# A decoder block on one core: the first norm's sums of squares are taken by ACT from token rows, and the first chunk's loads are cut anew

## The chip, the cores and the metric

The kernel runs on one NeuronCore of a Trainium2 chip. The metric is the device time of one execution in microseconds (us). Three runs of the kernel before took 1370.49, 1372.42 and 1373.44 us; the median is 1372.42. The names used below are those of the profile: PE is the matrix engine (TensorE), PEld its weight loads, DVE the vector engine, ACT the scalar engine, POOL the GpSimd engine, and SP the engine whose queue issues the transfers.

## The reference

One decoder block over 256 tokens of width 2048, in float32:

```
h = x + token_mixer(rmsnorm(x, norm1_w), ...)     # one input projection, retention and an SSD scan side by side,
                                                  # one output projection
h = h + hier_moe(rmsnorm(h, norm2_w), ...)        # 32 experts in 4 groups, two per token, gated MLPs
return rmsnorm(h, final_norm_w)

def rmsnorm(x, w):
    y = x * rsqrt(mean(x * x, axis=-1) + 1e-6)
    return y * w
```

What matters here is the first `rmsnorm`: for each of the 256 tokens a sum of squares over 2048 channels, and from it one factor per token. The input projection is linear in each token, so the factor can be applied after it.

## The kernel before, in words

Tokens lie in two halves of 128. The 2048 channels are 16 tiles of 128 (KT = 16). The input projection is done in 13 chunks of 512 output columns; each chunk is a loop over the 16 channel tiles. A tile's weights (128 x 512) are split into two float32r parts, a rounded one (`wh`, on ACT) and the rest (`wl`, on DVE), and six products of 512 columns (or twelve of 256) go to PE per tile: wh with xh, wl with xh, wh with xl. The split input (`xh` on ACT, `xl` on DVE, named `twin` for the first eight tiles) is made once, in the first chunk, by `prep_x`; it carries the norm's weight but not the factor per token. Each `wh`/`wl` pair has six buffers (two pools of three, STAGE = 6), so ACT and DVE can be at most six tiles ahead of PE.

Weights come in pieces of 8 tiles (2 MB) into a ring of two buffers (RING_A = 2); the transfer of a chunk's first half therefore waits until DVE has made the last `wl` of the half that lay in that buffer. All transfers stand in one queue, SP's, in order: one that waits holds up those behind it. In the first chunk the two halves are loaded in smaller pieces, each with the piece of x that goes with it (`first_tiles`).

The factor per token is made by `rms1`, which is taken up beside the second chunk by `pump` (a list of pieces of work, one of which is recorded after every second tile). `squares` has POOL square the 16 tiles of x (4 tiles at a time) and add them up; PE sums over the channels (`psr`); DVE and POOL make `rcol`, one factor per token on partitions; DVE and PE spread it over columns (`dg`, `psb`, `rbc`). `keep_v` takes the first chunk's result out of PSUM with `rcol` (ACT, tile `v`).

A scheduler turns this into a fixed order of instructions for each engine; an instruction that waits holds up everything behind it on its engine.

After the 13 chunks come the output projection, the routing, and eight groups of four experts. The experts' weights come in 192 pieces of 2 MB (some 400 MB of the 485 MB that the kernel moves), through rings of 2 MB buffers, on the same SP queue (`wload` and `stream`, L774); a piece is asked for when PE has used up the buffer it goes to.

Of the kernel before, what the change touches and what calls it, by code (L numbers as in the profile page):

```python
# [9 lines left out]
F32 = mybir.dt.float32  # L10
# [3 lines left out]
AF = mybir.ActivationFunctionType  # L14
# [4 lines left out]
P = 128  # L19
D = 2048  # L20
T = 256
NT = T // P
# [15 lines left out]
SPLIT = 1  # L38
# [111 lines left out]
def block_kernel(tc, I, out):  # L150
    nc = tc.nc
    act, dve, pe, pool, sp = nc.scalar, nc.vector, nc.tensor, nc.gpsimd, nc.sync
    MUL, ADD, SUB, MAX, MIN = ALU.mult, ALU.add, ALU.subtract, ALU.max, ALU.min
    EQ = ALU.is_equal

    def tt(o, a, b, op):
        dve.tensor_tensor(o, a, b, op=op)  # L157

    def stt(o, a, s, b, op0, op1, **k):
        dve.scalar_tensor_tensor(o, a, s, b, op0=op0, op1=op1, **k)  # L160

    def ts(o, a, s1, s2, op0, op1=None):
        if op1 is None:
            dve.tensor_scalar(o, a, s1, None, op0=op0)
        else:
            dve.tensor_scalar(o, a, s1, s2, op0=op0, op1=op1)

    def sb(name, side="left", bufs=1, **k):
        return tc.alloc_tile_pool(name=name, bufs=bufs, side=side, **k)
# [3 lines left out]
    par = cp.tile([P, PARAM.n], F32, name="par")  # L173

    def V(name):
        t, (o, n) = (par, PARAM.at[name]) if name in PARAM.at else (mxp, MIXP.at[name])
        return t[:, o:o + n]

    def C(name):
        t, (o, n) = (con, CONST.at[name]) if name in CONST.at else (mxc, MIXC.at[name])  # L180
        return t[:, o:o + n]
# [3 lines left out]
    sm = sb("small")  # L185
# [15 lines left out]
    ones = mp.tile([P, P], F32, name="ones")  # L201
    dve.memset(ones, 1.0)

    def twin(i, n, dt=F32):
        return qp.tile([P, 2, n, 2048 // n], dt, tag=f"h{i}", name=f"twin{i}")

    def t1(name, dt=F32, shape=(P, T)):
        return mp.tile(list(shape), dt, tag="t1", bufs=6, name=name)
# [4 lines left out]
    def misc(shape, name):  # L213
        return pm.tile(shape, F32, tag="pm", name=name)

    def rsqrt_mean(o, ss, n, tag):
        m = sm.tile(list(ss.shape), F32, name="rm" + tag)
        ts(m, ss, 1.0 / n, EPS, MUL, ADD)
        pool.tensor_tensor(o, m, mh[:, :ss.shape[1]], op=ALU.pow)
# [9 lines left out]
    xraw = hp.tile([P, KT, T], F32, tag="h", name="xraw")  # L229
# [3 lines left out]
    n1 = V("n1")  # L233

    def xh(k):
        return xhs[k // 8][:, k % 8]

    def xl(k):
        return xls[k // 8][:, k % 8]

    def load_x(a, b):
        sp.dma_start(xraw[:, a:b], I["xt"][:, a:b])

    def prep_x(a, b):
        for k in range(a, b):
            act.activation(xh(k), xraw[:, k], AF.Copy, scale=n1[:, k:k + 1])
            stt(xl(k), xraw[:, k], n1[:, k:k + 1], xh(k).bitcast(F32), MUL, SUB)

    rcol = cp.tile([P, NT], F32, name="rcol")
    lowb = cp.tile([P, P], BF16, name="lowb")  # L250
    onb = cp.tile([P, P], BF16, name="onb")
    pool.memset(onb, 1.0)
    rbc = mp.tile([P, T], F32, name="rbc")
    sq = t1("sq")

    def squares():

        ab = twin(1, 8)
        a, b = ab[:, 0, :4], ab[:, 1, :4]
        for i in range(4):  # L260
            xr = xraw[:, 4 * i:4 * i + 4]
            pool.tensor_tensor(b if i else a, xr, xr, op=MUL)
            if i:
                pool.tensor_tensor(a, a, b, op=ADD)
        pool.tensor_tensor(a[:, :2], a[:, :2], a[:, 2:], op=ADD)
        pool.tensor_tensor(sq, a[:, 0], a[:, 1], op=ADD)

    def rms1():
        squares()
        yield  # L270

        ps = misc([P, NT], "psr")
        for t in range(NT):
            pe.matmul(ps[:, t:t + 1], sq[:, t * P:(t + 1) * P], ones[:, :1], start=(t == 0), stop=True,
                      skip_group_check=True)
        rsqrt_mean(rcol, ps, D, "1")
        dg = t1("dg", shape=(P, NT, P))
        ps = misc([P, T], "psb")
        for t in range(NT):
            ts(dg[:, t], ident, rcol[:, t:t + 1], None, MUL)  # L280
        pe.matmul(ps, ones, dg.rearrange("p a b -> p (a b)"), start=True, stop=True)
        dve.tensor_copy(rbc, ps)
        yield
        sp.dma_start(mxp, I["mixp"])
        sp.dma_start(mxc, I["mixc"])
        sp.dma_start(wdt[:, :KT], I["wdt"])
        act.activation(lowb, C("strict"), AF.Copy)

    def split(w, n):
        for i in range(0, w.shape[1], n):  # L290
            st = stages.pop(0)
            stages.append(st)
            wh = st.tile([P, n, 512], F32R, tag="wh", name="wh")
            wl = st.tile([P, n, 512], F32R, tag="wl", name="wl")
            act.activation(wh, w[:, i:i + n], AF.Copy)  # L295
            tt(wl, w[:, i:i + n], wh.bitcast(F32), SUB)
            for j in range(n):
                yield i + j, wh[:, j], wl[:, j]

    def load(src):  # L300
        w = ring.tile([P, 8, 512], F32, tag="w", name="w")
        sp.dma_start(w, src)
        return w
# [23 lines left out]
                    pass  # L327

    def first_tiles():
        sp.dma_start(par, I["par"])  # L330
        for i, parts in enumerate((((0, 1), (1, 2), (2, 4), (4, 6), (6, 8)), ((0, 2), (2, 4), (4, 6), (6, 8)))):
            w = ring.tile([P, 8, 512], F32, tag="w", name="w")
            for a, b in parts:
                load_x(8 * i + a, 8 * i + b)
                sp.dma_start(w[:, a:b], I["win"][0, i, :, a:b])
            if i == 1:
                sp.dma_start(con, I["con"])
            for a, b in parts:
                prep_x(8 * i + a, 8 * i + b)
                for j, wh, wl in split(w[:, a:b], SPLIT):  # L340
                    yield 8 * i + a + j, wh, wl

    def win_tiles(ci):
        if ci == 0:
            yield from first_tiles()
            return
        for i in range(2):
            for j, wh, wl in split(load(I["win"][ci, i]), SPLIT):
                yield 8 * i + j, wh, wl

    def form_b(ci):
        ps = [pa.tile([P, 2, T], F32, tag="pa", name="pb") for _ in range(2)]
        for k, wh, wl in win_tiles(ci):
            for c in range(4):
                o = ps[c // 2][:, c % 2]
                s = slice(c * P, (c + 1) * P)
                pe.matmul(o, wh[:, s], xh(k), start=(k == 0 and c % 2 == 0), stop=False, skip_group_check=True)  # L357
                pe.matmul(o, wh[:, s], xl(k), start=False, stop=False, skip_group_check=True)  # L358
                pe.matmul(o, wl[:, s], xh(k), start=False, stop=(k == KT - 1), skip_group_check=True)  # L359
            if k % 2:  # L360
                pump(rate)
        return ps

    def form_a(tiles, lh, ll):
        ps = [pa.tile([P, 512], F32, tag="pa", name="pf") for _ in range(NT)]
        for k, wh, wl in tiles:
            for t in range(NT):
                s = slice(t * P, (t + 1) * P)
                pe.matmul(ps[t], lh(k)[:, s], wh, start=(k == 0), stop=False)  # L369
                pe.matmul(ps[t], lh(k)[:, s], wl, start=False, stop=False)  # L370
                pe.matmul(ps[t], ll(k)[:, s], wh, start=False, stop=(k == KT - 1))  # L371
            if k % 2:
                pump(rate)
        return ps
# [280 lines left out]
    for ci, (n, half) in enumerate(CHUNKS):  # L655
        rate = 2 if (n, half) == ("z", 0) else 1
        if n in ("xs", "bc", "q", "k"):
            ps = form_b(ci)
        else:
            ps = form_a(win_tiles(ci), xh, xl)  # L660
        finish_all(soon)
        if ci == 0:
            soon.append(rms1())
# [88 lines left out]
    op = sb("outp", side="right", reuse_waits="tile")  # L752
# [411 lines left out]
```

## Time and profile before

| | |
|---|---|
| median of 3 runs | 1372.42 us (1370.49 to 1373.44) |
| the profiled execution's own time | 1369.11 us |
| its span | 1367.3 us |
| PE busy | 1051.8 us (77%) |
| DVE busy | 415.9 us (30%) |
| ACT busy | 271.4 us (20%) |
| POOL busy | 25.6 us (2%) |
| DMA | 484.93 MB, mean 355 GB/s |
| mean granted clock of PE | 0.899 of full speed |

The span is what the trace covers; the execution takes 1.8 us more. A row of the timeline view gives a start and a length in us, then engine, line, operation and tile; "x2" means two instructions merged, and a bracket gives the idle time of the engine before it and what ended it. A granted clock of 1.00 is 2.4 GHz, 0.50 is 1.2 GHz.

### The profile page before, as it was taken

How to read it: one execution, taken by the hardware profiler on the slowest of the kernel's cores; microseconds unless marked ns; L12 is line 12 of the kernel's file. 1: busy time of each engine (PE TensorE's matmuls, PEld its weight loads, DVE VectorE, ACT ScalarE, POOL GpSimd, SP SyncE). 2: the span in 40 equal slices, each digit the busy share in tenths (PEclk: the TensorE clock that was granted, in tenths of full speed). 3: DMA queues.
4: the chain of work that ended last, by engine and by line, in shares of the span. 5: the costliest groups of instructions: out<-in, count | busy, mean ns of one | idle time of the engine just before them, and what ended most of it. 6: DMA issues, size and time to landing. Idle time of an engine off the chain costs nothing.

```text
span 1367.3 us, 17274 instructions
## 1 busy us (share of the span) xinstructions
PE 1051.8 (77%) x7323; PEld 597.3 (44%) x7323; DVE 415.9 (30%) x842; ACT 271.4 (20%) x504; POOL 25.6 (2%) x29
## 2 busy tenths in 40 slices
PE   6999999999999997667558567665865766595654
PEld 4889999888787542133113213211320321141112
DVE  8577977665655321011002101100200110020013
ACT  5465544465544100000000000000000000000003
POOL 5000000000000000000000000000000000000000
PEclk9999999999999998789889978978987896798888
DMA  7445555585875999999999999999999999999995
GB/s 264 177 151 189 192 193 202 195 323 193 327 301 223 365 426 427 427 427 427 428 427 426 426 429 426 425 427 428 428 425 427 426 427 428 427 427 426 428 425 222
DMA packets 38723, 484.93 MB, mean 355 GB/s; under 512 B 4561, under 2 KB 5233, under 8 KB 9585
## 3 DMA queue, kind: packets, MB, share of 16 engines
q1 hardware_dynamic: 38642, 483.78, 86.0%
q8 instruction: 59, 0.97, 0.3%
q14 instruction: 22, 0.18, 0.0%
HBM read 481.65 MB, written 2.11 MB: 354 GB/s over the span
## 4 chain that ended last, share of the span: by engine, by line
DMA 63%; PE 34%; DVE 1%; issue 1%; ACT 0%; SPq 0%; POOL 0%; POOLq 0%; DVEq 0%; ACTq 0%
DMA wt<-wexp 39%; DMA twin<-wexp 23%; PE pb L357 4%; PE pb L359 4%; PE pb L358 4%; PE pf L370 3%; PE pf L371 3%; PE pf L369 3%; PE po L729 2%; PE po L727 2%; PE po L728 2%; PE pg L973 1%; PE pu L973 1%; PE pxg L947 1%; DMA w<-win 1%
## 5 line engine op out<-in xcount | busy, mean ns | idle before, releaser
L973 PE MATMUL pu<-wt,xg 128*32 128x512 f32 x864 | 144.3, 798 | 95.9 <-DMA wt<-wexp 95.9
L973 PE MATMUL pg<-wt,xg 128*32 128x512 f32 x832 | 135.7, 782 | 84.3 <-DMA wt<-wexp 84.2
L157 DVE TENSOR_TENSOR wl<-w,wh 128x512 fp32r<-128x512 f32 x224 | 157.9, 717 | 73.0 <-ACT wh L295 71.6
L295 ACT ACTIVATE wh<-w 128x512 fp32r<-128x512 f32 x224 | 139.7, 630 | 149.2 <-PE pb L358 77.0
L157 DVE TENSOR_TENSOR sg<-sg,pu 128x512 f32<-128x512 f32 x8 | 5.5, 688 | 537.5 <-PE pu L973 536.3
L973 PE MATMUL py<-wt,at 128*32 128x128 f32 (+1 forms) x1456 | 112.7, 418 | 19.0 <-DMA wt<-wexp 19.0
L973 PEld LDWEIGHTS pu<-wt,xg 128*32 128x32 f32 x864 | 28.8, 129 | 208.5 <-DMA wt<-wexp 157.3
L973 PEld LDWEIGHTS pg<-wt,xg 128*32 128x32 f32 x832 | 25.8, 127 | 182.5 <-DMA wt<-wexp 136.2
L157 DVE TENSOR_TENSOR acc<-acc,psc 128x128 f32<-128x128 f32 (+1 forms) x98 | 43.3, 459 | 170.4 <-PE psc L1004 170.3
L1004 PE MATMUL psc<-y,swt 128*128 128x128 f32 (+1 forms) x224 | 70.8, 439 | 25.9 <-ACT y L1001 25.1
L973 PEld LDWEIGHTS py<-wt,at 128*32 128x32 f32 x1456 | 42.0, 110 | 78.6 <-issue 35.6
L1001 ACT ACTIVATE y<-py 128x128 f32<-128x128 f32 (+1 forms) x56 | 23.2, 414 | 233.3 <-PE py L973 233.2
L958 ACT ACTIVATE swt<-psw 128x256 f32<-128x256 f32 x8 | 3.1, 383 | 324.6 <-PE psw L956 324.6
L357 PE MATMUL pb<-twin,wh 128*128 128x256 f32 x224 | 64.4, 288 | 0.6 <-ACT wh L295 0.6
L359 PE MATMUL pb<-twin,wl 128*128 128x256 f32 x224 | 64.2, 288 | 0.0
L357 PE MATMUL pb<-xh,wh 128*128 128x256 f32 x224 | 64.2, 286 | 0.0
L358 PE MATMUL pb<-twin,wh 128*128 128x256 f32 x224 | 64.0, 286 | 0.0
L1004 PEld LDWEIGHTS psc<-y,swt 128*128 128x128 f32 x224 | 33.3, 192 | 67.9 <-ACT y L1001 56.3
L947 PEld LDWEIGHTS pxg<-selr,h 128*128 128x128 f32 x512 | 60.0, 196 | 6.5 <-issue 5.9
L359 PE MATMUL pb<-xh,wl 128*128 128x256 f32 x224 | 62.8, 280 | 0.0
L358 PE MATMUL pb<-xl,wh 128*128 128x256 f32 x224 | 62.7, 280 | 0.0
L990 ACT ACTIVATE sg<-pg 128x512 f32<-128x512 f32 x8 | 4.8, 597 | 291.4 <-PE pg L973 291.4
(259 smaller groups left out, 1479.2 us busy)
## 6 DMA issues: line engine op xcount, KB each, us to landing
wt<-wexp SPq DMA_DIRECT2D x156, 2048.0 KB, 39.1
twin<-wexp SPq DMA_DIRECT2D x34, 2048.0 KB, 39.1
w<-win SPq DMA_DIRECT2D x24, 2048.0 KB, 7.9
wt<-wout SPq DMA_DIRECT2D x6, 2048.0 KB, 12.3
w<-wout SPq DMA_DIRECT2D x2, 2048.0 KB, 7.8
wt<-wexp SPq DMA_DIRECT2D x4, 1024.0 KB, 31.9
w<-win SPq DMA_DIRECT2D x7, 512.0 KB, 8.1
de<-acd SPq DMA_DIRECT2D x8, 256.0 KB, 3.3
```

The source lines that it names most:

```text
L157: dve.tensor_tensor(o, a, b, op=op)
L295: act.activation(wh, w[:, i:i + n], AF.Copy)
L357: pe.matmul(o, wh[:, s], xh(k), start=(k == 0 and c % 2 == 0), stop=False, skip_group_check=True)
L358: pe.matmul(o, wh[:, s], xl(k), start=False, stop=False, skip_group_check=True)
L359: pe.matmul(o, wl[:, s], xh(k), start=False, stop=(k == KT - 1), skip_group_check=True)
L369: pe.matmul(ps[t], lh(k)[:, s], wh, start=(k == 0), stop=False)
L370: pe.matmul(ps[t], lh(k)[:, s], wl, start=False, stop=False)
L371: pe.matmul(ps[t], ll(k)[:, s], wh, start=False, stop=(k == KT - 1))
L727: pe.matmul(ps[t], yh[:, s], wh, start=(k == 0), stop=False)
L947: pe.matmul(px[:, i], h[:, t, (k0 + i) * P:(k0 + i + 1) * P], selr[:, t], start=(i == 0 and x == 0), stop=(x == NT - 1), skip_group_check= ...
L973: pe.matmul(ps[s], lhsT[:, s], w(j), **k)
L1004: pe.matmul(px, swt[:, t * P:(t + 1) * P], y, start=True, stop=True)
```

## The change

The tile `sq` and the function `squares` go, and with them POOL's nine large operations at the start and PE's product `psr`. Instead x is loaded a second time, by token rows (`xtok`, 2 MB, 128 partitions x 4096), behind the first weights of the second chunk on SP's queue; ACT squares it in place in four instructions of 128 x 1024, each leaving a sum (`accum_out`) in `ss1`; DVE adds the two halves (`ssum`), and the rest of `rms1` stands as it was.

The first chunk's loads have 12 pieces instead of 18. The parameters (`par`) and the first weight tile are issued by ACT; all others by SP.

```diff
-    def prep_x(a, b):
-        for k in range(a, b):
-            act.activation(xh(k), xraw[:, k], AF.Copy, scale=n1[:, k:k + 1])
-            stt(xl(k), xraw[:, k], n1[:, k:k + 1], xh(k).bitcast(F32), MUL, SUB)
+    def prep_x(k):
+        act.activation(xh(k), xraw[:, k], AF.Copy, scale=n1[:, k:k + 1])
+        stt(xl(k), xraw[:, k], n1[:, k:k + 1], xh(k).bitcast(F32), MUL, SUB)
...
-    sq = t1("sq")
-
-    def squares():
-
-        ab = twin(1, 8)
-        a, b = ab[:, 0, :4], ab[:, 1, :4]
-        for i in range(4):
-            xr = xraw[:, 4 * i:4 * i + 4]
-            pool.tensor_tensor(b if i else a, xr, xr, op=MUL)
-            if i:
-                pool.tensor_tensor(a, a, b, op=ADD)
-        pool.tensor_tensor(a[:, :2], a[:, :2], a[:, 2:], op=ADD)
-        pool.tensor_tensor(sq, a[:, 0], a[:, 1], op=ADD)
+    xtok = twin(1, 1)[:, :, 0]
+    ss1 = sm.tile([P, NT, 2], F32, name="ss1")
+    ssum = sm.tile([P, NT], F32, name="ssum")
 
     def rms1():
-        squares()
-        yield
-
-        ps = misc([P, NT], "psr")
+
         for t in range(NT):
-            pe.matmul(ps[:, t:t + 1], sq[:, t * P:(t + 1) * P], ones[:, :1], start=(t == 0), stop=True,
-                      skip_group_check=True)
-        rsqrt_mean(rcol, ps, D, "1")
+            for i in range(2):
+                row = xtok[:, t, 1024 * i:1024 * i + 1024]
+                act.activation(row, row, AF.Square, accum_out=ss1[:, t, i:i + 1])
+            yield
+
+        tt(ssum, ss1[:, :, 0], ss1[:, :, 1], ADD)
+        rsqrt_mean(rcol, ssum, D, "1")
...
     def first_tiles():
-        sp.dma_start(par, I["par"])
-        for i, parts in enumerate((((0, 1), (1, 2), (2, 4), (4, 6), (6, 8)), ((0, 2), (2, 4), (4, 6), (6, 8)))):
+        for i, parts in enumerate((((0, 1), (1, 2), (2, 4), (4, 8)), ((0, 4), (4, 8)))):
             w = ring.tile([P, 8, 512], F32, tag="w", name="w")
+            if i == 0:
+                act.dma_start(par, I["par"])
             for a, b in parts:
                 load_x(8 * i + a, 8 * i + b)
-                sp.dma_start(w[:, a:b], I["win"][0, i, :, a:b])
+                (sp if i or a else act).dma_start(w[:, a:b], I["win"][0, i, :, a:b])
...
     def win_tiles(ci):
...
         for i in range(2):
-            for j, wh, wl in split(load(I["win"][ci, i]), SPLIT):
+            w = load(I["win"][ci, i])
+            if ci == 1 and i == 0:
+                sp.dma_start(xtok, I["x"])
+            for j, wh, wl in split(w, SPLIT):
                 yield 8 * i + j, wh, wl
```

On SP's queue, around the end of the first chunk's loads, there stood before (`xraw` is x by channels, `w` the weights, 128x4096 is a whole 2 MB piece; L302 is the load of a later chunk's half):

```order
L335 DMA w<-win 128x1024
L242 DMA xraw<-xt 128x512
L335 DMA w<-win 128x1024
L337 DMA con<-con 128x160
L302 DMA w<-win 128x4096
L284 DMA mxp<-mixp 128x108
L285 DMA mxc<-mixc 128x1289
L286 DMA wdt<-wdt 128x256
L302 DMA w<-win 128x4096 x8
```

And now, from the fourth transfer of the queue on (L326 is the first chunk's weights, `twin_126` is `xtok`):

```order
L242 DMA xraw<-xt 128x512
L326 DMA w<-win 128x1024
L242 DMA xraw<-xt 128x1024
L326 DMA w<-win 128x2048
L242 DMA xraw<-xt 128x1024
L326 DMA w<-win 128x2048
L328 DMA con<-con 128x160
L292 DMA w<-win 128x4096
L341 DMA twin_126<-x 128x4096
L274 DMA mxp<-mixp 128x108
L275 DMA mxc<-mixc 128x1289
L276 DMA wdt<-wdt 128x256
```

From the fifth tile on the pieces hold four tiles instead of two, and the second load of x stands between the second chunk's first weights and the three small transfers.

On ACT, from the first chunk's last tiles into the second chunk, there stood before (`v` is the first chunk's result leaving PSUM, which waits for `rcol`):

```order
L246 ACTIVATE xh_119<-xraw,par 128x256 x2
L295 ACTIVATE wh<-w 128x512 x2
L563 ACTIVATE v<-pf,rcol 128x512 x2
L295 ACTIVATE wh<-w 128x512 x6
L287 ACTIVATE lowb<-mxc 128x128
```

And now (L262 are the four squares; twelve `wh` are the first chunk's last four and the second chunk's first eight):

```order
L245 ACTIVATE xh_119<-xraw,par 128x256 x4
L285 ACTIVATE wh<-w 128x512 x12
L262 ACTIVATE twin_126,ss_127<-twin_126 128x1024 x4
L277 ACTIVATE lowb<-mxc 128x128
L438 ACTIVATE aex<-mxp 128x16
L557 ACTIVATE v<-pf,rcol 128x512 x2
L285 ACTIVATE wh<-w 128x512 x16
```

The instruction that waits for `rcol` has moved from the head of the second chunk to its middle, behind eight of its sixteen tiles, and the squares stand just ahead of it.

On PE, where the factor is spread over columns, there stood before (`pf` is the first chunk's sum, `pb` the second's):

```order
L370 MATMUL pf<-wl,xh_119 128x512
L371 MATMUL pf<-wh,xl_120 128x512
L274 MATMUL psr<-ones,sq 128x1 x2
L281 MATMUL psb<-dg,ones 128x256
L357 MATMUL pb<-twin_118,wh 128x256
```

And now:

```order
L353 MATMUL pb<-twin_118,wl 128x256
L271 MATMUL psb<-dg,ones 128x256
L351 MATMUL pb<-twin_118,wh 128x256
L352 MATMUL pb<-twin_118,wh 128x256
L353 MATMUL pb<-twin_118,wl 128x256
```

`psb` has moved from between the two chunks to behind 90 of the second chunk's 192 products (7.5 of its 16 tiles), and `psr` is gone.

## Rows read from the trace of the kernel before

**Rows 1.** The page's chain that ended last, by engine.
```profile
DMA 63%; PE 34%; DVE 1%; issue 1%; ACT 0%; SPq 0%; POOL 0%; POOLq 0%; DVEq 0%; ACTq 0%
```

**Rows 2.** Windows: start:end, length, each engine's busy us (instructions), PE clock, DMA, GB/s.
```profile
410.00:448.00 38.00, 37.47 (x196) 28.10 (x195) 21.10 (x50) 18.06 (x33) 1.24 (x3) 1.00 0.62 227
465.00:500.00 35.00, 34.13 (x292) 17.69 (x291) 8.87 (x25) 0.98 (x2) 0.00 (x0) 1.00 1.01 428
```

**Rows 3.** Waits of SP's queue from 440 to 500 us (total, times, longest).
```profile
SPq L774 <- PE pg L973: 25.3, 7, 9.8
```

**Rows 4.** Timeline of PE: the two first chunks' beginnings and stalls.
```profile
5.54 0.73 PE L369 MATMUL pf<-wh,twin 128*128 128x512 f32 x2
...
23.80 0.79 PE L370 MATMUL pf<-wl,twin 128*128 128x512 f32 x1 [5.64 <-DVE wl L157]
...
31.16 0.51 PE L370 MATMUL pf<-wl,xh 128*128 128x512 f32 x1 [1.88 <-DVE wl L157]
...
42.24 0.50 PE L274 MATMUL psr<-ones,sq 128*128 128x1 f32 x4
44.30 0.70 PE L281 MATMUL psb<-dg,ones 128*128 128x256 f32 x2 [1.56 <-DVE dg L164]
45.60 0.38 PE L357 MATMUL pb<-twin,wh 128*128 128x256 f32 x1 [0.60 <-ACT wh L295]
...
70.23 0.39 PE L369 MATMUL pf<-wh,twin 128*128 128x512 f32 x1
```

**Rows 5.** Timeline of DVE, same work with POOL busy and without.
```profile
20.92 5.12 DVE L157 TENSOR_TENSOR wl<-w,wh 128x512 fp32r<-128x512 f32 x2
...
32.43 1.28 DVE L157 TENSOR_TENSOR wl<-w,wh 128x512 fp32r<-128x512 f32 x2
```

**Rows 6.** Timeline of POOL beside it.
```profile
20.80 2.40 POOL L264 TENSOR_TENSOR twin<-twin 128x1024 f32<-128x1024 f32 x1
23.27 2.22 POOL L262 TENSOR_TENSOR twin<-xraw 128x1024 f32<-128x1024 f32 x1
```

**Rows 7.** Windows after two of PE's gaps: the clock.
```profile
24.00:26.00 2.00, 2.00 (x5) 1.61 (x6) 2.00 (x2) 0.00 (x0) 1.92 (x2) 0.50 0.00 0
46.00:48.00 2.00, 2.00 (x11) 1.81 (x11) 2.00 (x5) 2.00 (x5) 0.00 (x0) 0.60 0.01 4
```

**Rows 8.** Windows over the first loads: the last column is GB/s.
```profile
0.00:8.00 8.00, 6.16 (x17) 2.36 (x17) 2.07 (x6) 3.74 (x7) 0.61 (x10) 1.00 0.64 189
8.00:10.00 2.00, 1.90 (x6) 0.93 (x6) 2.00 (x2) 0.82 (x2) 1.95 (x1) 1.00 0.99 317
10.00:12.00 2.00, 0.76 (x3) 0.33 (x3) 1.84 (x4) 1.44 (x3) 0.39 (x1) 1.00 1.01 386
12.00:20.00 8.00, 5.79 (x23) 4.13 (x23) 7.86 (x7) 7.63 (x17) 6.35 (x3) 1.00 1.03 405
```

**Rows 9.** Timeline of ACT: two pieces of weights landing, and the wait for `rcol`.
```profile
10.56 1.15 ACT L295 ACTIVATE wh<-w 128x512 fp32r<-128x512 f32 x2 [1.74 <-DMA w<-win]
...
12.78 0.63 ACT L295 ACTIVATE wh<-w 128x512 fp32r<-128x512 f32 x1 [0.27 <-DMA w<-win]
...
43.76 0.69 ACT L563 ACTIVATE v<-pf,rcol 128x512 f32<-128x512 f32 x1 [9.09 <-POOL rcol L219]
```

**Rows 10.** Timeline of SP: the second chunk's first weights.
```profile
26.07 0.33 SPq L302 DMA_DIRECT2D w<-win  x1
```

**Rows 11.** ACT's squares with a sum elsewhere, by form (busy us, mean ns).
```profile
L1086 ACT ACTIVATE sg<-acc 128x512 f32<-128x512 f32 x6 | 3.8, 631 | 8.4 <-DVE acc L157 8.4
L1086 ACT ACTIVATION_READ_ACCUMULATOR sg<-acc 128x1 f32 x14 | 2.6, 187 | 0.0
...
L1086 ACT ACTIVATE sg<-acc 128x128 f32<-128x128 f32 x8 | 2.5, 308 | 2.3 <-DVE acc L157 2.2
```

**Rows 12.** Timeline of DVE: from the sums to the spread factor.
```profile
42.78 0.16 DVE L166 TENSOR_SCALAR rm<-psr 128x2 f32<-128x2 f32 x1 [5.07 <-PE psr L274]
...
45.04 0.43 DVE L282 COPY rbc<-psb 128x256 f32<-128x256 f32 x1 [0.79 <-PE psb L281]
```

More of the change, by code (lines that the diff above doesn't have):

```diff
@@ L329, in first_tiles @@
     def first_tiles():
-        sp.dma_start(par, I["par"])
-        for i, parts in enumerate((((0, 1), (1, 2), (2, 4), (4, 6), (6, 8)), ((0, 2), (2, 4), (4, 6), (6, 8)))):
+        for i, parts in enumerate((((0, 1), (1, 2), (2, 4), (4, 8)), ((0, 4), (4, 8)))):
             w = ring.tile([P, 8, 512], F32, tag="w", name="w")
+            if i == 0:
+                act.dma_start(par, I["par"])
             for a, b in parts:
                 load_x(8 * i + a, 8 * i + b)
-                sp.dma_start(w[:, a:b], I["win"][0, i, :, a:b])
+                (sp if i or a else act).dma_start(w[:, a:b], I["win"][0, i, :, a:b])
             if i == 1:
                 sp.dma_start(con, I["con"])
[L338 to L341, printed above, removed]
+            for k in range(8):
+                prep_x(8 * i + k)
+                for _, wh, wl in split(w[:, k:k + 1], 1):
+                    yield 8 * i + k, wh, wl
     def win_tiles(ci):
```

## The prediction, made before the changed kernel ran

> **What bounds the kernel now.** I read the chain of waits first [rows 1]: 63% of the span is DMA and 34% PE. Windows tell where each rules. Until 448 us PE is busy nearly without a break and DMA moves only 227 GB/s; from 465 us on DMA moves 428 GB/s and stays there [rows 2]. The experts' stream does not start by itself: SP's queue waits for PE to free buffers [rows 3]. So the end is a PE-bound front of about 450 us plus a fixed stream, and a microsecond saved in the front, wherever PE is the last to finish, moves the end by one microsecond.
>
> The change is all in the first 70 us. There PE is not full [rows 4]: the first chunk's products begin at 5.54 and end at 42.24, the second chunk's begin at 45.60 and end at 70.23. What a full chunk takes is read from the last eight tiles of the first: from 31.16 to 42.24, 11.08 us, 47 of their 48 products ran, 0.236 us each, so a tile of six takes 1.41 and a chunk of sixteen 22.6. (The second chunk has twice as many products of half the length, so the same.) The first chunk takes 36.7, the second 24.6.
>
> Why: the longest stalls, 5.64 and 1.88 us, end on DVE's `wl` [rows 4]. DVE does two `wl` in 5.12 us while POOL squares and adds, and two in 1.28 us once POOL has stopped [rows 5, 6]. After the 5.64 us gap the granted clock is 0.50, that is 1.2 GHz instead of 2.4; after the gap from 42 to 45.6 it is 0.60 [rows 7]. That second gap is `rms1` itself: PE stands until `dg` is there, and ACT waited 9.09 us for `rcol` with the second chunk's weights behind it [rows 4, 9].
>
> **The change part by part.**
>
> *POOL's nine operations go.* With them goes DVE's slowness; DVE then needs 0.64 per `wl` [rows 5], well under PE's 1.41 per tile, and the first chunk is set by its loads and by PE. How loads land: a tile's x and weights are 0.393 MB, `par` 0.043. By 8 us 1.51 MB had moved, then 317 and 386 GB/s [rows 8]. The weights of tiles 2 and 3 (1.62 MB in all) had moved at 8.3 and were used at 10.56; those of tiles 4 and 5 (2.40 MB) had moved at 10.7 and were used at 12.78 [rows 8, 9]. So transfers land in order, 2.1 to 2.2 us after their last byte.
>
> *The recut.* Now tile 4 waits for all of tiles 4 to 7, 3.19 MB. I take the same curve, 0.4 us earlier, since `par` has left the head of SP's queue: 1.62 MB at 7.9, the next 1.57 MB at 400 GB/s (between the 386 and 405 of rows 8) 3.9 us: 11.8, plus 2.1 is 13.9. `wh` takes about 0.6 (half of 1.15 in rows 9), so tile 4 begins at 14.6 and tile 15 ends at 14.6 + 12 x 1.41 = 31.5. The next piece lands 3.9 later, at 17.8, when PE is at its seventh tile; it is hidden, and so is the last. What ACT issues itself changes nothing here, since tile 4 waits for its own piece in any case. Bounds: if only the weights of tiles 2 and 3 bind, at 10.2, the end is 10.2 + 14 x 1.41 = 29.9; if the loads go on at the mean rate up to tile 5 (2.40 MB in 10.7 us, 225 GB/s), 33.8. Against 42.24 the term is **10.7 us** (8.4 to 12.3). Set against small pieces, the recut costs about one microsecond of this, hidden in the sum.
>
> *The pause between the chunks goes.* `psr` is gone, `psb` and ACT's wait for `rcol` stand in the second chunk's middle. From 42.24 to 45.60 are 3.4 us; `psb` itself, 0.7 [rows 4], comes back: **2.7 us**. The second chunk's first weights must be there: their transfer went out at 26.07, when DVE had done tile 7 [rows 10]. Now that is 13.9 + 0.6 + 4 x 0.64, about 17.2; they move from about 19.8, when the first chunk's 6.4 MB are through, to 24.7 at 428 GB/s [rows 2], and are there at 26.8, before 31.5.
>
> *The clock.* With no gap before it, the second chunk runs at 22.6 instead of 24.6: **2.0 us** (0 if the gap at tile 4 costs the clock instead; it is estimated at about a microsecond, and after the 1.88 us gap PE was back at 0.236 per product).
>
> *The squares on ACT, a new wait.* `xtok` moves behind those weights, 24.7 to 29.6, and is there at 31.7. ACT comes to the squares when it has made the second chunk's eighth `wh`; six buffers mean that PE must have done the second tile: 31.5 + 2.8 + 0.6 = 34.9. So `xtok` is early by 3 us. A square of 128 columns takes 308 ns and of 512 takes 631 [rows 11], 0.84 ns a column, so 1024 take 1.06, plus 0.19 to read the sum; bounds are 0.63 (no growth) and 1.26 (twice the row). Four are 5.0, to 39.9. Behind them wait `v` and the second half's `wh` on ACT, the second half's `wl` on DVE (behind `ssum`, `rm`, `dg`, `rbc`), and all of PE at `psb`. From `rm` to the end of `rbc` took 2.7 us [rows 12]; with `ssum` 2.9: 42.8, and `wl` of tile 8 is ready at 43.5. PE reaches `psb` at 31.5 + 7.5 x 1.41 = 42.1, and tile 8 at 43.5; there it wants `wl` with its fourth product. I take a hole of **0.5 us** (0 to 2.2: four squares cost 5.0 or 5.8, 1.2 more if `psb` comes late). The 2 MB more of traffic fall in the front, where DMA has room (227 against 428 GB/s [rows 2]).
>
> **Sum:** 10.7 + 2.7 + 2.0 - 0.5 = 14.9 us. The profiled execution took 1369.1 (span 1367.3 and 1.8 around it): 1354.2. The median of the runs shown is 3.3 above the profiled one, so for a median **1357.5**; own range 1354 to 1362.
>
> **A rule to weigh.** A transfer lands 2.1 to 2.2 us after its bytes [rows 8, 9], while the first 8 us moved only 189 GB/s [rows 8]. The Trainium skill, DMA: Bandwidth & Descriptors (Anatomy of one DMA), puts a transfer at about 2.0 us plus its bytes at 436 GB/s, the fixed part mostly the wait until the last byte is confirmed. The trace agrees on the fixed part and not on the rate. By that rule the 3.19 MB would be there near 10 us and nothing but PE would bind the chunk.
>
> **Rivals.**
>
> *The larger pieces move at full rate from 2 us on.* For it: 405 GB/s once the stream runs [rows 8]. Against: no row reaches it before 10 us. Tile 4's piece would land at 2.0 + 3.19/0.405 + 2.1 = 12.0, the chunk end at 29.5, 2.0 better: 1355.5. (The rule above points this way.)
>
> *The squares come late.* If loads ran at the 317 GB/s of 8 to 10 us throughout, tile 4's piece would land at 15.0 (1.1 later) and `xtok` (10.6 MB in all) at 38.3, 3.4 after ACT is ready; PE then stands about 4 us and loses up to 2 to the clock: gain 8.4, 1364. Against: 405 and 428 in the later rows.
>
> *Nothing comes of it.* The stream would start no earlier because something other than PE paces it. Against: SP waits for PE [rows 3], and DMA has room before 448. 1372.
>
> *Slower.* One place can do it: `psb` and ACT's `v` stand in order in the second chunk's middle, so every microsecond that `xtok` lands after 34.9 is one that PE stands. The saving of 14.9 is used up when it lands near 48 (the clock takes 2 more); at 53 the time is 1377. The 4.2 MB behind 19.8 us would have to move at 160 GB/s, below the 189 of the slowest row [rows 8].
>
> **How the numbers follow.** Forecast 0.70, full rate 0.10, late squares 0.12, nothing 0.05, slower 0.03. About 0.2%, 2.7 us, can be told from no change here: faster 0.92, same 0.05, slower 0.03. The range runs from the full-rate case, less what runs scatter, to the late squares: 1352 to 1365.
>
> **What would show it.** DVE's `wl` at 0.64 to 0.7 throughout, no `wl` wait over a microsecond; tile 4's `wh` near 14; the second chunk's first product near 31.5 and the third chunk's near 55, against 70.23; clock 1.00 through both; `xtok` landed before ACT's eighth `wh` of the second chunk; the experts' stages as long as before. It is wrong if DVE stays slow without POOL, if PE stands at tile 8 for microseconds, or if the third chunk starts 15 us earlier and the end does not.

## The result, and the profile after

The changed kernel takes 1355.62 us (median of 4 runs, 1354.11 to 1356.53); the kernel before took 1371.45 beside it (4 runs, 1370.40 to 1373.44). The ratio is 0.9882, interval 0.9867 to 0.9898. The profiled execution took 1354.11 with a span of 1352.3, against 1369.1 and 1367.3: 15.0 us less, where the sum had said 14.9.

The page's chain and totals (busy us, share of the span, instructions) first. POOL has 6.7 us left of 25.6, and DVE is busy for 14.6 us less (401.3 against 415.9); PE changes little.

```profile
PE 1048.4 (78%) x7319; PEld 597.4 (44%) x7319; DVE 401.3 (30%) x843; ACT 275.2 (20%) x512; POOL 6.7 (0%) x20
...
DMA 61%; PE 37%; DVE 0%; issue 0%; ACT 0%; SPq 0%; POOLq 0%; POOL 0%; DVEq 0%; ACTq 0%
```

The end is still a PE-bound front and a fixed stream. These are the windows of [rows 2], 15 us earlier: PE's busy times are the same, and DMA moves 228 and 429 GB/s where it moved 227 and 428.

```profile
395.00:433.00 38.00, 37.47 (x196) 28.10 (x195) 21.09 (x50) 18.08 (x33) 1.24 (x3) 1.00 0.62 228
450.00:485.00 35.00, 34.13 (x292) 17.69 (x291) 8.87 (x25) 0.98 (x2) 0.00 (x0) 1.00 1.01 429
```

PE's timeline against [rows 4]. The stalls of 5.64 and 1.88 us on `wl` are gone; tile 4 starts at 13.21 after 0.48 us of waiting, the first chunk ends at 30.32 (42.24 before) and the second begins there without a pause; `psb` stands in its middle; the third chunk starts at 54.06 (70.23).

```profile
12.34 0.39 PE L365 MATMUL pf<-wh,twin 128*128 128x512 f32 x1
13.21 0.73 PE L363 MATMUL pf<-wh,twin 128*128 128x512 f32 x2 [0.48 <-ACT wh L285]
...
30.09 0.40 PE L365 MATMUL pf<-wh,xl 128*128 128x512 f32 x1
30.32 0.28 PE L351 MATMUL pb<-twin,wh 128*128 128x256 f32 x1
...
41.10 0.60 PE L271 MATMUL psb<-dg,ones 128*128 128x256 f32 x2
...
42.48 0.28 PE L351 MATMUL pb<-xh,wh 128*128 128x256 f32 x1
42.81 0.39 PE L353 MATMUL pb<-xh,wl 128*128 128x256 f32 x1
...
54.06 0.40 PE L363 MATMUL pf<-wh,twin 128*128 128x512 f32 x1
```

The `pb` of 42.81 stands 0.33 us behind the one before it instead of 0.12, and the next, at 43.03, another 0.22 behind it: these 0.3 us beyond the usual 0.12 are all that is left of a hole at the squares.

DVE, grouped by form from 0 to 44 us (count, busy us, mean ns, idle before): every `wl` takes 0.69 us and DVE waits for ACT's `wh`, not the other way round. In [rows 5], beside POOL's work, two took 5.12.

```profile
L157 DVE TENSOR_TENSOR wl<-w,wh 128x512 fp32r<-128x512 f32 x28 | 18.0, 687 | 8.8 <-ACT wh L285 8.8
```

ACT's timeline: tile 4's weights are split from 12.53; the four squares begin at 33.80 with no wait for their load, 1.04 us apart, with the read of a sum (0.19) overlapped; `v` follows at 39.34 after 0.98 us for `rcol`, against 9.09 in [rows 9].

```profile
12.53 2.19 ACT L285 ACTIVATE wh<-w 128x512 fp32r<-128x512 f32 x4 [0.80 <-DMA w<-win]
...
33.80 1.04 ACT L262 ACTIVATE twin<-twin 128x1024 f32<-128x1024 f32 x1
...
37.87 0.19 ACT L262 ACTIVATION_READ_ACCUMULATOR twin<-twin 128x1 f32 x1
...
39.34 1.27 ACT L557 ACTIVATE v<-pf,rcol 128x512 f32<-128x512 f32 x2 [0.98 <-POOL rcol L219]
```

The windows of the first loads, answering [rows 8] and [rows 7]: more is moved early than before (227 GB/s against 189, then 434 against 317), and the granted clock is 1.00 in every window, also around the chunk's change and `psb`.

```profile
0.00:8.00 8.00, 6.45 (x17) 2.49 (x17) 2.67 (x6) 4.20 (x8) 0.61 (x10) 1.00 0.72 227
8.00:10.00 2.00, 1.91 (x7) 1.16 (x7) 1.47 (x4) 1.52 (x3) 0.00 (x0) 1.00 1.07 434
10.00:12.00 2.00, 2.00 (x9) 1.54 (x9) 2.00 (x6) 1.71 (x4) 0.00 (x0) 1.00 0.97 403
...
28.00:34.00 6.00, 6.00 (x42) 5.54 (x41) 2.85 (x5) 2.98 (x6) 0.00 (x0) 1.00 1.03 417
41.00:45.00 4.00, 3.95 (x32) 3.69 (x31) 3.27 (x6) 3.36 (x7) 0.00 (x0) 1.00 0.10 39
```

### The profile page after: what moved, and what is told of

It reads as the page before. It is cut to its first block, busy times and chain, and to the rows that moved or that the text cites. A ratio compares the mean times of both kernels' runs of the same rounds, so it can differ in the third digit from the quotient of the medians.

```text
span 1352.3 us, 17251 instructions
## 1 busy us (share of the span) xinstructions
PE 1048.4 (78%) x7319; PEld 597.4 (44%) x7319; DVE 401.3 (30%) x843; ACT 275.2 (20%) x512; POOL 6.7 (0%) x20
## 4 chain that ended last, share of the span: by engine, by line
DMA 61%; PE 37%; DVE 0%; issue 0%; ACT 0%; SPq 0%; POOLq 0%; POOL 0%; DVEq 0%; ACTq 0%
DMA wt<-wexp 40%; DMA twin<-wexp 20%; PE pb L353 4%; PE pb L351 4%; PE pb L352 4%; PE pf L363 3%; PE pf L364 3%; PE pf L365 3%; PE po L723 2%; PE po L721 2%; PE po L722 2%; PE py L967 1%; PE pu L967 1%; PE pxg L941 1%; PE pg L967 1%; PE psc L998 1%
## 5 line engine op out<-in xcount | busy, mean ns | idle before, releaser
L157 DVE TENSOR_TENSOR wl<-w,wh 128x512 fp32r<-128x512 f32 x224 | 151.3, 689 | 72.6 <-ACT wh L285 71.8
L967 PE MATMUL py<-wt,at 128*32 128x128 f32 (+1 forms) x1456 | 115.7, 427 | 17.9 <-DMA wt<-wexp 17.7
L941 PE MATMUL pxg<-selr,h 128*128 128x128 f32 x512 | 63.1, 284 | 0.6 <-DVE selr L164 0.6
## 6 DMA issues: line engine op xcount, KB each, us to landing
w<-win SPq DMA_DIRECT2D x3, 1024.0 KB, 11.3
twin<-x SPq DMA_DIRECT2D x1, 2048.0 KB, 14.9
```

Of the source, the lines that this page charges most:

```text
L941: pe.matmul(px[:, i], h[:, t, (k0 + i) * P:(k0 + i + 1) * P], selr[:, t], start=(i == 0 and x == 0), stop=(x == NT - 1), skip_group_check= ...
L967: pe.matmul(ps[s], lhsT[:, s], w(j), **k)
```

## The experiments

Six points of PE's timeline carry the comparisons: the end of the first chunk, the start of the third, the first `pcb` and `po` products (retention, output projection), the first `pxg` (routing), and the span, all in us of the profiled executions. The median of each kernel stands last, in us.

| kernel | first ends | third starts | to `pcb` | `pcb` to `po` | `po` to `pxg` | span | median |
|---|---|---|---|---|---|---|---|
| before | 42.24 | 70.23 | 115.8 | 159.9 | 105.5 | 1367.3 | 1371.45 |
| after | 30.32 | 54.06 | 116.6 | 160.2 | 105.5 | 1352.3 | 1355.62 |
| recut only | 44.15 | 67.78 | 115.7 | 160.0 | 105.5 | 1364.5 | 1366.87 |
| squares only | 31.09 | 54.84 | 116.7 | 160.3 | 107.1 | 1354.5 | 1355.99 |
| no squares | 32.45 | 57.04 | 115.8 | 159.9 | 105.5 | 1353.9 | 1355.66 |
| POOL's work back | 43.77 | 67.51 | 116.7 | 160.3 | 107.1 | 1368.5 | 1368.82 |
| second load late | 30.05 | 59.25 | 116.7 | 160.3 | 107.1 | 1359.5 | 1361.28 |
| squares twice | 29.68 | 57.26 | 115.8 | 159.8 | 108.7 | 1358.7 | 1359.04 |
| all issues on SP | 31.88 | 55.63 | 116.7 | 160.3 | 108.3 | 1359.1 | 1358.50 |
| POOL only writes | 30.07 | 53.81 | 116.6 | 160.3 | 105.5 | 1352.5 | 1356.16 |
| old cut, ACT issues | 28.95 | 52.70 | 116.6 | 160.3 | 105.5 | 1350.8 | 1353.40 |
| more issues on ACT | 31.45 | 55.95 | 116.6 | 160.3 | 105.5 | 1355.2 | 1357.39 |
| only `par` on ACT | 31.87 | 55.61 | 116.7 | 160.3 | 107.1 | 1355.8 | 1356.90 |
| best, shifted 32 bytes | 28.75 | 52.31 | 115.8 | 159.9 | 105.5 | 1349.2 | 1352.19 |

The column `po` to `pxg` varies from 105.5 to 108.7 in a stage that no edit touches, so differences of a microsecond or two are read at the third chunk's start, not from the span. Four kernels have the changed kernel's first chunk unaltered (after, second load late, squares twice, POOL only writes); it ends between 29.68 and 30.32 there, which is how far one execution can be trusted.

**1. The recut alone** (the kernel before with the new `first_tiles`, ACT's two issues included, and the new `prep_x`; the edit's main line).

```diff
...
-        for i, parts in enumerate((((0, 1), (1, 2), (2, 4), (4, 6), (6, 8)), ((0, 2), (2, 4), (4, 6), (6, 8)))):
+        for i, parts in enumerate((((0, 1), (1, 2), (2, 4), (4, 8)), ((0, 4), (4, 8)))):
...
```

> The kernel before with only the first chunk's loads cut anew and the two issues on ACT; POOL still squares. (The scheduler now puts psb some four tiles into the second chunk and the copies that wait for rcol behind ten of the wh.) Theory A (the time was lost because POOL's operations slow DVE, and a smaller part in the pause between the chunks): wl still takes over 2 us while POOL works, the first chunk still ends at 40 to 43 us, and only the pause and its clock go: 2 to 5 us faster than before, 1367 to 1370. Theory B (the recut loads are what made it faster): 10 us or more faster, under 1362, the first chunk ending near 32.

1366.87, ratio 0.9970 (0.9952 to 0.9988). The first chunk ends later than before, and later than the 40 to 43 us expected: pieces of four tiles put four low parts of x in a row on DVE beside POOL's work, and PE waits 7.35 us at once instead of 5.64.

```profile
14.96 9.12 DVE L160 SCALAR_TENSOR_TENSOR twin<-xraw,par,twin 128x256 fp32r<-128x256 f32 x4
```
```profile
25.80 0.79 PE L370 MATMUL pf<-wl,twin 128*128 128x512 f32 x1 [7.35 <-DVE wl L157]
```

What it gains (2.45 us at the third chunk) is the pause: `psr` and `psb` have slipped into the second chunk, at 44.61 and 50.33.

**2. The squares alone** (the change with the old 18 pieces, all issued by SP; the loads as in the kernel before).

> The squares from token rows on ACT, with the old cut of the first loads in 18 pieces, all issued by SP. Theory A: as fast as the whole change within 1 us or so, 1354 to 1357; the first chunk ends between 29.5 and 31.5. Theory B: at most 5 us faster than before, 1367 or more.

1355.99, ratio 0.9884 (0.9859 to 0.9909): nearly the whole gain.

**3. No squares at all**, in the kernel before: the factor is a constant for all tokens.

```diff
-        squares()
+        pool.memset(sq, 16.0)
```

> The kernel before with POOL's squares and sums left out: sq is filled with a constant, so the factor per token is the same for all tokens; loads and order as before, and the copies waiting for rcol still stand ahead of the second chunk's wh on ACT. Theory A: wl at 0.65 to 0.7 us throughout, the first chunk ends at 29.5 to 31 (11 to 12.5 us earlier); of the pause about 2 us stay, because the copies must wait for the end of the first chunk: 13 to 15 us faster, 1356 to 1359. Theory C (most of the gain is the pause and the clock, not DVE): under 6 us faster.

PE's timeline, between the first two chunks:

```profile
32.45 0.59 PE L281 MATMUL psb<-dg,ones 128*128 128x256 f32 x2
33.91 0.38 PE L357 MATMUL pb<-twin,wh 128*128 128x256 f32 x1 [0.86 <-ACT wh L295]
```

1355.66, ratio 0.9879 (0.9858 to 0.9900). Taking POOL's work away gives 13.19 us at the third chunk; the loads stay as before, and `psb` between the chunks too, where 0.86 us of a pause are left. Of the 13.19, 9.79 are the first chunk's: it ends at 32.45, not at the 29.5 to 31 expected. PE had waited 2.04 us for tile 2's weights, and behind that wait its granted clock was 0.50:

```profile
12.00:14.00 2.00, 2.00 (x5) 1.61 (x6) 1.94 (x5) 1.81 (x4) 0.00 (x0) 0.50 1.04 415
```

**4. POOL's work put back into the changed kernel**: seven operations that read x and write a tile that nothing else reads.

```diff
+    spare = mp.tile([P, 4, T], F32, name="spare")
+    def idle_squares():
+        for i in range(4):
+            xr = xraw[:, 4 * i:4 * i + 4]
+            pool.tensor_tensor(spare, xr, xr, op=MUL)
+            if i:
+                pool.tensor_tensor(spare, spare, xr, op=ADD)
...
+        idle_squares()
```

> The changed kernel with seven POOL operations of 128 x 1024 that read x put back beside the first chunk, into a tile that nobody reads. Theory A: wl is back above 2 us while they run, the first chunk ends 7 to 12 us later than in the changed kernel, and the time is 1362 to 1368. Theory B: no change, 1354 to 1357.

1368.82, ratio 0.9973 (0.9961 to 0.9986): 13.45 us are lost at the third chunk, all of them in the first chunk (43.77 against 30.32), where 7 to 12 were expected. Nothing else waits for what these operations write, so it is their presence that costs. DVE's rows are those of experiment 1 again, and PE waits 6.30 us:

```profile
15.16 9.13 DVE L160 SCALAR_TENSOR_TENSOR twin<-xraw,par,twin 128x256 fp32r<-128x256 f32 x4
```
```profile
24.94 0.80 PE L375 MATMUL pf<-wl,twin 128*128 128x512 f32 x1 [6.30 <-DVE wl L157]
```

**5. POOL only writes**: 24 memsets of 128x1024 in the changed kernel, 23 of them without a pause.

```diff
+    spare = mp.tile([P, 4, T], F32, name="spare")
+    for _ in range(24):
+        pool.memset(spare, 1.0)
```

> The changed kernel with 24 POOL memsets of 128 x 1024 from the start (about 20 us by the size of the memsets in the trace), which write but read nothing. If what slows DVE is POOL being busy at all: wl back above 1.5 us and 5 us or more slower, 1361 or more. If it is POOL reading the same memory as DVE: wl stays at 0.69 and the time at 1354 to 1357.

1356.16, and the third chunk at 53.81. POOL is busy for 23 us and `wl` stays as quick as without it:

```profile
1.98 23.26 POOL L259 MEMSET spare<- 128x1024 f32 x23
```
```profile
L157 DVE TENSOR_TENSOR wl<-w,wh 128x512 fp32r<-128x512 f32 x28 | 18.0, 686 | 8.8 <-ACT wh L289 8.8
```

So POOL slows DVE here with operations that read SBUF, and not with ones that only write it. (A memset also computes less than a product; no run has POOL read without arithmetic.) The Trainium skill, SBUF — State Buffer (Who interferes with whom), says that a DVE instruction with two SBUF inputs contends with a GpSimd instruction that reads SBUF, not with one that only writes it; experiments 4 and 5 agree with both halves (2.28 us against 0.48 for a low part of x, 0.686 against 0.687 for `wl`).

**6. The second load late**: it is issued three times.

```diff
-                sp.dma_start(xtok, I["x"])
+                for _ in range(3):
+                    sp.dma_start(xtok, I["x"])
```

> The changed kernel with the load of the token rows issued three times in a row into the same tile, so that the last lands some 15 us later (near 45 us), and SP's queue is held up meanwhile; the scheduler now puts the squares behind all sixteen wh of the second chunk and psb near its end. Theory A (only the place of the wait for rcol among the other work counts): the squares end near 50 us, as the second chunk ends; 0 to 4 us slower than the changed kernel, 1355 to 1359. Theory D (every microsecond that the rows land late is one that PE stands): 8 us slower or more, 1363 or more.

1361.28, ratio 0.9933 (0.9910 to 0.9955). 5.7 us above the changed kernel, between the two theories' ranges. It missed its aim: the squares stand behind all sixteen `wh` and PE does not wait for them. The 5.2 us at the third chunk were lost elsewhere, at the second half's weights, held up on SP's queue behind the extra loads, and at the clock behind that wait (0.50 from 46 to 48 us):

```profile
44.91 3.23 ACT L285 ACTIVATE wh<-w 128x512 fp32r<-128x512 f32 x6 [10.98 <-DMA w<-win]
```
```profile
45.59 0.58 PE L352 MATMUL pb<-xh,wh 128*128 128x256 f32 x1 [3.88 <-ACT wh L285]
```

So the run says nothing on late squares; it prices what is queued behind the load.

**7. Squares twice**: a second pass over each row.

```diff
+    ss0 = sm.tile([P, NT, 2], F32, name="ss0")
...
+                act.activation(row, row, AF.Copy, accum_out=ss0[:, t, i:i + 1])
                 act.activation(row, row, AF.Square, accum_out=ss1[:, t, i:i + 1])
```

> The changed kernel with four more ACT passes of 128 x 1024 with a sum (plain copies, in place) between the squares, 4.2 us more on ACT; psb stands six products later, the rest of the order as it was. Theory A (the squares have about a microsecond of slack before PE comes to psb, and beyond it ACT's time is PE's time): PE stands 3 to 4 us in the second chunk, 3 to 6 us slower than the changed kernel, 1358.5 to 1361.5. Theory E (ACT has room, the squares are hidden): no change, 1354 to 1357.

1359.04, ratio 0.9910 (0.9883 to 0.9936). Four passes more, 4.16 us of ACT, start the third chunk 3.2 us later (3.8 counted from the first chunk's end), 2.05 of it as a wait at `psb`. Most of the rest went behind that wait, at the clock: from 44 to 48 us 21 products ran, against 36 in the changed kernel. So about 2 of the 4.16 us were hidden, also because `psb` stands six products (0.7 us) later here. In the changed kernel itself `dg` is done at 39.82 and `psb` starts at 41.10: the squares have 1.3 us to spare.

```profile
43.41 0.70 PE L273 MATMUL psb<-dg,ones 128*128 128x256 f32 x2 [2.05 <-DVE dg L164]
```
```profile
44.00:46.00 2.00, 1.98 (x8) 1.62 (x8) 1.85 (x4) 2.00 (x5) 0.00 (x0) 0.56 0.00 0
46.00:48.00 2.00, 2.00 (x13) 2.00 (x12) 2.00 (x4) 1.77 (x4) 0.00 (x0) 0.58 0.04 8
```

**8. All first loads issued by SP.**

```diff
-                act.dma_start(par, I["par"])
+                sp.dma_start(par, I["par"])
...
-                (sp if i or a else act).dma_start(w[:, a:b], I["win"][0, i, :, a:b])
+                sp.dma_start(w[:, a:b], I["win"][0, i, :, a:b])
```

> The changed kernel with the parameters and the first weight tile issued by SP as before; the new cut stays. Theory A: the piece of tiles 4 to 7 lands 0.4 to 0.9 us later and the first chunk ends as much later; at most 1 us slower, which the timed runs can't tell from none: 1354.5 to 1357.5. Rival: two queues move the bytes faster, and 2 us or more are lost without.

The third chunk starts 1.57 us later than in the changed kernel, between theory A (at most 1) and its rival (2 or more). Tile 4's weights are split at 14.06 instead of 12.53. They went out on SP's queue 0.91 us later (4.50 against 3.59), which leaves 0.6 us that the issue's place alone does not give. The loads' rate between 6 and 8 us differs too; first this kernel, then the changed one:

```profile
6.00:8.00 2.00, 1.35 (x5) 0.67 (x4) 0.49 (x2) 0.48 (x1) 0.00 (x0) 1.00 0.69 202
```
```profile
6.00:8.00 2.00, 1.86 (x6) 0.86 (x5) 1.19 (x3) 1.17 (x3) 0.00 (x0) 1.00 1.01 377
```

Its median, 1358.50, is 2.9 above the changed kernel's, but its routing stage took 108.3 instead of 105.5.

**9. The old cut with ACT's two issues** (experiment 2 with `par` and the first weight tile on ACT; the main line of its edit of the changed kernel).

```diff
...
-        for i, parts in enumerate((((0, 1), (1, 2), (2, 4), (4, 8)), ((0, 4), (4, 8)))):
+        for i, parts in enumerate((((0, 1), (1, 2), (2, 4), (4, 6), (6, 8)), ((0, 2), (2, 4), (4, 6), (6, 8)))):
...
```

> The squares on ACT, the old cut in 18 pieces, but the parameters and the first weight tile issued by ACT. Theory F (ACT's two issues are worth about 1.5 us of the first chunk, the new cut costs about 0.8): the first chunk ends near 29.5 us and the third begins near 53.3 us, a little before the changed kernel's 30.3 and 54.1; timed 1353.5 to 1356. Theory G (the new cut and the issues only work together): the first chunk ends at 31 or later, as with the old cut on SP alone.

1353.40 (1352.60 to 1354.06), ratio 0.9862 (0.9842 to 0.9883). The third chunk starts 1.36 us before the changed kernel's, tile 4's weights are split at 10.91 (12.47 in experiment 2, where they went out 0.9 us later). The ratios' intervals overlap; only the traces, one execution each, separate the two.

**10 and 11. More and fewer issues on ACT**: the weights of tiles 1 to 3 as well; then `par` alone.

```diff
-                (sp if i or a else act).dma_start(w[:, a:b], I["win"][0, i, :, a:b])
+                (act if i == 0 and b <= 4 else sp).dma_start(w[:, a:b], I["win"][0, i, :, a:b])
```

> The changed kernel with three weight pieces (tiles 0, 1, and 2 with 3) on ACT's queue beside the parameters, x on SP's. Theory F: two queues move the first small pieces faster still; tile 4's wh begins near 12 and the first chunk ends at 29 to 30, at most 1 us better in time. Against it: ACT issues for 0.9 us longer before its first activation, and the first chunk ends no earlier than 30.3.

> The changed kernel with the first weight tile back on SP and only the parameters on ACT. If it is SP's issue time that counts (0.46 us for each transfer moved): tile 4's wh begins about half way, at 13.0 to 13.6, and the first chunk ends near 31. If it is the weights in a second queue: as with all on SP, tile 4's wh at 14 and the chunk end near 31.9.

1357.39 and 1356.90. Neither is better. With more issues, ACT's table load came after them and after the wait for x, so the first activation on x started at 4.72 instead of 3.40. The weights that ACT issued also landed later: those of tiles 1 and 2 were split at 8.22 and 10.73, after waits for their loads, against 6.67 and 8.75.

```profile
3.42 1.28 ACT L245 ACT_TABLE_LOAD   x1 [3.42 <-DMA xraw<-xt]
```

With `par` alone, tile 4's weights went out 0.46 us earlier than in experiment 8 and were split at 13.55, 0.51 earlier, which is what the issue's place gives; but after a gap of 1.97 us PE's granted clock was 0.53 from 11 to 14 us, and its chunk ended no earlier than with all on SP. So it is the move of the first weight tile that gains more than its issue takes, and why is open.

```profile
10.45 0.73 PE L363 MATMUL pf<-wh,twin 128*128 128x512 f32 x2 [1.97 <-ACT wh L285]
```
```profile
11.00:14.00 3.00, 3.00 (x8) 2.25 (x8) 2.30 (x6) 2.15 (x5) 0.00 (x0) 0.53 1.01 419
```

**12. The best version with a 16-byte tile more.** The table's fourth and fifth columns fall in two groups, and the groups are those of the buffers' addresses in the built programs: `wh` begins at 62784 in the kernel before, at 62848 in the changed one (two new small tiles stand ahead of it), at 62880 in "squares twice".

```diff
+    pad = sm.tile([P, NT, 2], F32, name="pad")
+    pool.memset(pad, 0.0)
```

> The version with the old cut and ACT's two issues (third chunk at 52.70 us, first pcb 116.6 us later, po another 160.3) with one unread tile of 16 bytes per partition among the small tiles, set once by POOL. In the built program it moves wh, wl, twin and xraw up by 32 bytes: wh begins at 62880 (remainder 32 by 128) instead of 62848 (remainder 0); before it began at 62784 (remainder 64). The runs so far split by that: third chunk's start to pcb takes 115.8 us in before, recut only, no squares (remainder 64) and squares twice (remainder 32), 116.6 in all the others (remainder 0); pcb to po 159.9 against 160.3. Theory P (the address of these buffers sets whether products come 0.1175 or 0.120 us apart, and that is the 1.2 us given back between 95 and 225 us): third chunk unchanged near 52.7, pcb 115.8 later, po 159.9 later, so po near 328.4 instead of 329.6, and a median 1.2 lower, near 1352.2. Rival Q (the order of work with the squares on ACT costs it, and squares twice escaped for another reason): 116.6 and 160.3 as before the tile, po near 329.6, median near 1353.4.

1352.19 (1351.02 to 1352.95), ratio 0.9860 (0.9840 to 0.9881). That is the lowest median, but the kernel before took 1370.97 beside it and 1373.16 beside experiment 9, whose ratio is 0.9862: the medians don't separate the two, and the reading rests on the traces. They show 115.8 and 159.9, as theory P said. Over 20 products from 97.8 us, in this kernel and in experiment 9, PE needs 2.36 us (0.118 each) and 2.40 (0.120 each):

```profile
97.80 0.28 PE L354 MATMUL pb<-xl,wh 128*128 128x256 f32 x1
...
100.16 0.28 PE L353 MATMUL pb<-xh,wh 128*128 128x256 f32 x1
```
```profile
97.78 0.28 PE L353 MATMUL pb<-xh,wl 128*128 128x256 f32 x1
...
100.18 0.28 PE L352 MATMUL pb<-xl,wh 128*128 128x256 f32 x1
```

Only the products with `xh` and `xl`, those of the last eight tiles, change. The ones with `twin` stand 0.120 us apart in this kernel as well (2.40 us for 20), and in the kernel before (0.1199 on average):

```profile
101.23 0.28 PE L353 MATMUL pb<-twin,wh 128*128 128x256 f32 x1
...
103.63 0.28 PE L355 MATMUL pb<-twin,wl 128*128 128x256 f32 x1
```

From the third chunk to `po` run 576 products with `xh` and `xl` (six chunks of 96); at 0.002 us each they make the 1.2 us. Experiments 1 to 4 ran on one chip and fall in both groups, so the chip is not the cause. `wh`, `wl`, `twin` and `xraw` move together, so the run shows that an address decides. No product reads `xraw`, and those of `twin` do not change, so what is left is where `wh` and `wl` begin beside `xh` and `xl`.

## Why the prediction was right

**What bounds the kernel** was right and is the base of the rest: the third chunk starts 16.2 us earlier, every later stage follows, and the end moves by 15.0. The rival that nothing comes of it is out, and so is the slower one: the squares had no DMA wait.

**POOL's nine operations.** The mechanism is shown from both sides (experiments 3 and 4: 9.79 and 13.45 us of the first chunk), and its condition by experiment 5. The term was mis-sized: 11.9 us (42.24 to 30.32) against 10.7, within its bounds of 8.4 to 12.3. The step that missed is the load curve, in two places. Tile 4 was put at 14.6, from pieces "0.4 us earlier" at 400 GB/s; it began at 13.21. With 377 GB/s between 6 and 8 us and 434 from 8 to 10, the 3.19 MB had moved by 11.3, not 11.8. And `wh` started at 12.53, at most 1.3 us after the last byte instead of 2.1. The 2.1 to 2.2 us read from the kernel before are no fixed price: they are upper bounds, since bytes of later pieces may have moved in between, and by the same reckoning it is 1.6 in experiment 8 and 0.8 in experiment 9. The fit that the prediction takes from the Trainium skill, DMA: Bandwidth & Descriptors (Anatomy of one DMA), is given there for transfers issued by GpSimd; these are issued by SP and ACT, and the changed kernel's 1.3 us does not bear out its fixed 2.0. The landing lies nearer to the full-rate rival's 12.0 than to the forecast's 13.9, and so does the first chunk's end (30.32; the rival 29.5, the forecast 31.5).

**"What ACT issues itself changes nothing here" was wrong.** Two issues on ACT are worth 1.6 to 2.2 us of the first chunk with the new cut (experiment 8, 31.88 against 29.68 to 30.32) and 2.14 with the old (31.09 to 28.95). The argument, that tile 4 waits for its own piece in any case, left out that this piece is issued and moved behind all the others.

**The recut's microsecond** fits, within what one execution shows: with the same issuer the new cut ends the first chunk 0.8 us later (31.88 against 31.09) or, with ACT's issues, 0.7 to 1.6 (29.68 to 30.32 against 28.75 and 28.95). With POOL still at work the whole recut, ACT's issues included, costs 1.9 (44.15 against 42.24).

**Pause, clock, hole.** From the first chunk's end to the third's start took 27.99 us and now takes 23.74: 4.25 less, against 2.7 + 2.0 - 0.5 = 4.2. The clock is 1.00 throughout. The hole is 0.3, not 0.5: four squares took 4.3 us instead of 5.0, since the reads of the sums overlap.

**What no step had: the addresses.** 16.2 at the third chunk became 15.0 at `po`: 0.8 are lost up to `pcb` and 0.3 to 0.4 up to `po`. Experiment 12 gets this back (0.8 and 0.4) with a tile of 16 bytes and no other edit of experiment 9, so it is a price of the change's new small tiles. It nearly cancels the 1.2 us by which the first term was too small, which is why the sum fits as closely as it does. That is luck: the total fits better than its parts.

**The median.** 3.3 us was added for the distance of median and profiled run; this time that distance was 1.5. That is the difference between 1357.5 and 1355.62.

**Open:** why the first loads run faster, by more than the issue's place gives, when two queues issue them; how the place of `wh` and `wl` beside `xh` and `xl` sets the pitch; and what makes the routing stage take 105.5 in some executions and up to 108.7 in others. There the clock dips, as in the window of "squares twice" (first row) against the changed kernel's:

```profile
422.00:442.00 20.00, 18.59 (x125) 14.64 (x123) 10.03 (x46) 7.52 (x18) 1.66 (x5) 0.83 0.75 277
```
```profile
422.00:442.00 20.00, 18.59 (x156) 13.10 (x159) 10.12 (x54) 7.45 (x16) 1.66 (x5) 1.00 0.83 315
```

## What to carry to other kernels

Work on an engine off the critical path is not free: look for a slow-down of its neighbour's instructions while it runs, as `wl` at 2.6 us beside POOL's reads and at 0.69 without. Judge an early stage at the next fixed point of the timeline, since a later stage's scatter can be larger than the effect. And where a total fits, compare it stage by stage: here two errors of 1.2 us hid each other.

## What the runs showed of the hardware beyond that

- POOL reading SBUF stretches DVE's two-input operations four- to fivefold (0.64 us per `wl` to 2.56 in [rows 5]; x's low parts from 0.48 to 2.28, experiment 4); POOL writing the same 23 us does nothing (0.686 against 0.687).
- Two of the first loads issued by ACT raise the rate between 6 and 8 us from 202 to 377 GB/s (experiment 8); over the first 8 us the changed kernel and experiments 1, 4, 5, 6, 7, 9 and 12, which have both issues on ACT, moved 220 to 244 GB/s, the kernel before and experiments 2, 3 and 8 168 to 189. The Trainium skill, Trainium Kernel Development and Optimization (Key Constraints), says that issuing from several engines saves only the sequencer's issue time; the two issues took 0.85 us on ACT, and the chunk gained at least 1.56, more than that, in one execution of each kernel; with `par` alone moved (experiment 11) the trace agrees.
- 128x256 products with `xh` and `xl` come 0.1175 to 0.118 us apart or 0.120, at a granted clock of 1.00, by where `wh` begins: remainders of 64 and 32 by 128 bytes are the quick ones, 0 the slow one (three addresses seen). Those with `twin`, which moves along, come 0.120 apart in every kernel.
- The same stage, `po` to `pxg`, takes 105.5, 107.1 or 108.3 to 108.7 us in different executions.
